# Where the low parts of the experts' weights are computed in an encoder block on one NeuronCore: on VectorE and GpSimd, or on VectorE alone

## The chip, the core and the metric

The kernel runs on one core of one Trainium2 chip. The metric is the device time of one execution in microseconds. The kernel before takes 2730.11 us (median of three runs, 2722.38 to 2731.14). One execution was recorded by the profiler; all views below are of that one.

## What is computed

An encoder block over 1024 tokens of width 1024: layer norm, input projection, two head groups (a recurrent one and a forgetting attention), output projection, layer norm, and then a mixture of experts. The last is where this study plays:

```python
logits = xt @ router_w + router_b
top_val, top_idx = lax.top_k(logits, 4)          # of 32 experts
gates = softmax(top_val)
hid = xb @ w1[e] + b1[e]                         # 1024 -> 2048, for the tokens xb of expert e
x_glu = minimum(hid[..., ::2], 7); x_lin = clip(hid[..., 1::2], -7, 7)
act = x_glu * sigmoid(1.702 * x_glu) * (x_lin + 1)
out = act @ w2[e] + b2[e]                        # 1024 -> 1024
y = sum over a token's experts of gate * out
```

A layer norm of the residual and y follows. All of it is in float32.

## The kernel before

The program has a projection stage, the two head groups, an output projection with the router, the expert stage (about 1043 to 2680 us of the profiled execution) and the last layer norm.

**Exact products from split numbers.** PE multiplies in a rounded float32 format. To keep the accuracy, each factor is split into a high part (a rounding cast) and a low part (the number less its high part), and three products are summed: high by high, high by low, low by high. For activations ScalarE casts the high part from PSUM and VectorE subtracts (`xh`, `xl`, `ah`, `al`, L1148 and L1149). For weights ScalarE casts `wh` from `raw` (L1178), and `wl` = `raw` - `wh` is subtracted at L1181.

**The stream of weights.** The weights of the 32 experts are 384 blocks of [128, 2048] (1 MB each): eight blocks for an expert's first product, four for its second. `weights(j, ahead)` gives block j. It issues loads up to six blocks ahead (`RB`) on SyncE's queue, and it issues the casts and subtractions of the blocks up to j + 3 (`AH`) ahead of block j's matmuls. `wh` and `wl` have four buffers each (`WB`), so the cast of a block waits until PE has done with the block four before. Which engine subtracts is set by a set `pool` of block numbers, from two lists of places in an expert, `POOL_H` and `POOL_L`: 113 of the 384 go to GpSimd, the rest to VectorE.

**Slots and extra slots.** Each expert gets 128 slots for tokens. The 18 experts with the most tokens (`NH`) get 32 extra slots (`CX`); the order of the experts (`SEQ`) spreads these among the others. The extra rows don't use split factors: PE multiplies them straight from `raw` with 32 columns (`ex`, L1199 and L1253). Blocks of tokens beyond the slots are handled by a loop at the end.

**Turns.** The expert stage is written out by hand, without a scheduler. Turn r is the first product of expert r (`up`, eight blocks, steps 0 to 7), then the second product of expert r-1 (`down`, four blocks, steps 8 to 11). Small work is hung on steps: `plan(r, where, f)` puts f behind block `where` of turn r. The activation of expert r has a part for the extra rows (`gx`, `lx`, straight after the first product), and two halves (`gm`, `lm`; L1215 to L1219) at steps 8 and 9 (`DP`), each of which reads half of the first product's PSUM (`h`). Its transposes follow at steps 11, 13 and 14 (`TP`). The next turn's first matmuls (L1190, the bias by a one-hot `sel`) write `h` again and so wait until both halves have been read.

The slots of expert r+2 are worked out in turn r. `begin2` at step 6 makes the one-hot `oh` (L1135) and `sel` (L254). `third` at step 8 (`SLP`) has PE sum what is in the slots (`slots`, L1015 and L1021), VectorE copy it out (`st`, L1030, `sv`, L1005) and compute row numbers, and GpSimd gather the tokens (L1010). For an expert with extra slots, `extra` then turns the extra slots' values (L1027, a matmul that reads `st`), again with `sv`, row numbers and a gather behind it. It stands `SLE` = 1 step later, at step 9. All these matmuls and the transposes write the same PSUM tile `tr`, one buffer, so each waits until the one before has been read.

**Queues.** Every engine works in the order in which its instructions were issued. GpSimd has the subtractions of its blocks, the gathers, and the adding scatters of the results (L1271, L1280).

**The biases of the first product** are split into three exact bfloat16 parts before the expert stage (L259 to L269): two halves of 1024 columns, each with three copies of the biases on 96 partitions. GpSimd subtracts, ScalarE casts, on one group of 32 partitions at a time.

Of the kernel before, what the change touches and what calls it, by code (L numbers as in the profile page):

```python
# [14 lines left out]
OP = mybir.AluOpType  # L15
# [20 lines left out]
NE = 32  # L36
# [4 lines left out]
# the order of work, as ranks by falling count: those with extra slots spread among the others  # L41
SEQ = (0, *sorted(range(1, NE - 1), key=lambda r: (r + 0.5) / NH if r < NH else (r - NH + 0.5) / (NE - NH)), NE - 1)
# the expert that comes first whatever its count, so that its weights can be there early
# [4 lines left out]
SLE = 1  # L48
# [16 lines left out]
POOL_H = (2, 8, 9, 11)  # L65
POOL_L = (0, 10, 11)
# [5 lines left out]
def hybrid_kernel(ctx: ExitStack, tc: tile.TileContext, A, out):  # L72
# [179 lines left out]
    def select(pick):  # L252
        sel = wr.tile([96, P], BF, name="sel", bufs=2)
        ve.tensor_scalar(sel, ons, pick, None, op0=OP.mult)  # L254
        return sel

    first_sel = select(lead_pick)
    # biases of the experts' first product in three exact parts, on 0..31, 32..63 and 64..95
    bh = wr.tile([96, 2 * FF], BF, name="bh")  # L259
    for i in range(2):  # L260
        q = slice(i * FF, (i + 1) * FF)
        b1 = wr.tile([96, FF], FT, name="b1", tag=("xg", "xe")[i])
        for g in range(3):
            sp.dma_start(b1[32 * g:32 * g + 32], A["b1"][:, q])
        ac.copy(bh[:, q], b1)
        for g in (1, 2, 2):
            z = slice(32 * g, 32 * g + 32)
            gp.tensor_tensor(b1[z], b1[z], bh[z, q], op=OP.subtract)
            ac.copy(bh[z, q], b1[z])  # L269
# [14 lines left out]
def rsqrt_steps(nc, pool, v, n, scale, eps, name="rq", out=None):  # L284
    """(v * scale + eps) ** -0.5 for a small tile, one step a call: a first guess from the exponent, then three
    Newton steps r * (3 - a * r * r) / 2, whose factors -2, -8 and -512 are left to the end."""
    ve = nc.vector
    a, r, t = (pool.tile([P, n], FT, name=f"{name}_{x}") for x in "art")
    ve.tensor_scalar(a, v, scale, eps, op0=OP.mult, op1=OP.add)  # L289
    yield r  # L290
    ve.tensor_scalar(r.bitcast(I32), a.bitcast(I32), -0.5, 1597463007.0, op0=OP.mult, op1=OP.add)  # L291
    yield
    for c in (3.0, 12.0, 768.0):
        if n == 1:
            ve.scalar_tensor_tensor(t, r, a[:, 0:1], r, op0=OP.mult, op1=OP.mult)
        else:
            ve.tensor_tensor(t, r, r, op=OP.mult)  # L297
            yield
            ve.tensor_tensor(t, t, a, op=OP.mult)  # L299
        yield  # L300
        ve.scalar_tensor_tensor(r, t, c, r, op0=OP.subtract, op1=OP.mult)  # L301
        yield
    ve.tensor_scalar(r, r, -1.0 / 8192.0, None, op0=OP.mult)
    yield
# [10 lines left out]
def layer_norm2(nc, pool, x, w, b, name, bufs=2):  # L315
    """Layer norm with the scaling on the scalar engine and the last addition on GpSimd."""
    ve = nc.vector
    stt = pool.tile([P, 2, 6], FT, name="ln_st")
    ve.bn_stats(stt[:, 0], x[:, 0:512])
    ve.bn_stats(stt[:, 1], x[:, 512:1024])  # L320
    mv = pool.tile([P, 2], FT, name="ln_mv")
    ve.bn_aggr(mv, stt)
    rs = rsqrt(nc, pool, mv[:, 1:2], 1, 1.0, LN_EPS)
    nm = pool.tile([P, 1], FT, name="ln_nm")
    ve.scalar_tensor_tensor(nm, mv[:, 0:1], -1.0, rs, op0=OP.mult, op1=OP.mult)
    h = pool.tile([P, D], FT, name=name, bufs=bufs)
    nc.scalar.activation(h, x, AF.Identity, bias=nm, scale=rs)
    ve.tensor_tensor(h, h, w, op=OP.mult)
    nc.gpsimd.tensor_tensor(h, h, b, op=OP.add)
    return h  # L330
# [161 lines left out]
def rw_prep(tc, A, L):  # L492
# [16 lines left out]
    # columns at or after the row (inclusive), then strictly after  # L509
# [37 lines left out]
    # inverses of the 16-wide diagonal blocks, four blocks a partition  # L547
# [265 lines left out]
def post_mix(tc, A, L):  # L813
# [60 lines left out]
    def half():  # L874
# [16 lines left out]
        # on 0..31 and 32..63 the high parts, on 64..95 the low ones  # L891
# [22 lines left out]
    def route(t, h1):  # L914
# [29 lines left out]
        # position of the token among those of its expert  # L944
# [13 lines left out]
        # the gate in three exact parts  # L958
# [8 lines left out]
    def rest(t, h1, G):  # L967
        """The sum's start: the residual and the gated biases."""
        n = slice(t * P, (t + 1) * P)
        b2 = L["b2"]  # L970
        ps = ps3.tile([96, P], FT, name="sm")
        for i in range(3):
            pe.matmul(ps[32 * i:32 * i + 32], G, ident, start=True, stop=True)
        gt = p3.tile([96, P], FR, name="gt")
        ac.copy(gt, ps)
        ve.tensor_tensor(gt[32:64], ps[32:64], f32(gt)[32:64], op=OP.subtract)
        yi = p3.tile([P, D], FT, name="yi", bufs=YIB)
        for c in range(2):
            q = slice(512 * c, 512 * c + 512)
            ps = ps3.tile([P, 512], FT, name="sm")  # L980
            pe.matmul(ps, gt, b2[:, q], start=True, stop=True)
            ve.scalar_tensor_tensor(yi[:, q], h1[:, q], ALPHA, ps, op0=OP.mult, op1=OP.add)
        sp.dma_start(ya_d[n, :], yi)
# [5 lines left out]
    # rows beyond the tokens, one a slot, for the slots nobody fills  # L989
# [7 lines left out]
    def slots(pv, oh, n, pq, tag, wr):  # L997
        """What the slots of an expert hold: gates, rows of the tokens, the tokens."""
# [19 lines left out]
        if nh == 2:  # L1018
# [5 lines left out]
            def extra():  # L1024
                """Four copies of the extra slots, one to a group of columns."""
                ps = pq.tile([P, 6], FT, name="slots", tag=tag)
                pe.matmul(ps, st.rearrange("c g s -> c (g s)"), ident[0:6, 0:6], start=True, stop=True)  # L1027
                fill(ps, 1, xe, CX)
# [20 lines left out]
    def rank():  # L1049
        """Experts by falling count, with FIRST before all."""  # L1050
# [10 lines left out]
        # bt[e, f]: e goes before f  # L1061
# [21 lines left out]
    def table():  # L1083
        """Blocks of tokens beyond the slots: partition i holds the expert and the first position of block i."""
# [30 lines left out]
def experts(tc, A, L):  # L1115
# [3 lines left out]
    with ExitStack() as cx:  # L1119
# [18 lines left out]
        def turn(src, name):  # L1138
            """Pieces of work that transpose [128, 1024] and split it into high and low parts."""
# [25 lines left out]
        stream, raws, highs, ready, pool = [], L["raws"], L["highs"], [], set()  # L1165

        def weights(j, ahead):
            """Block j of the stream; loads and splits run ahead of it."""
# [4 lines left out]
            while len(ready) < min(j + 1 + ahead, len(stream)):  # L1173
# [7 lines left out]
                (gp if i in pool else ve).tensor_tensor(l, raw, f32(h), op=OP.subtract)  # L1181
# [39 lines left out]
        def act(ps, px):  # L1221
            """Pieces of work, two halves and the extra rows, each followed by its transposes."""
# [103 lines left out]
        for r in range(NE + 1):  # L1326
            if r < NE:
                at["u", r] = len(stream)
                pool |= {len(stream) + k for k in (POOL_H if SEQ[r] < NH else POOL_L) if k < KD}
                stream += [lambda r=r, k=k: w1(expert(r))(k) for k in range(KD)]  # L1330
            if r:
                at["d", r - 1] = len(stream)
                if r < NE:
                    pool |= {len(stream) + k - KD for k in (POOL_H if SEQ[r - 1] < NH else POOL_L) if k >= KD}
                stream += [lambda r=r, b=b: w2(expert(r - 1))(b) for b in range(4)]
        with tc.manual_schedule():
            info[0] = None, None, CAP, L["first_sel"]
            pool.add(0)
# [45 lines left out]
        # blocks beyond the slots, as many as the routing left  # L1384
        n = nc.values_load(L["tot"][0:1, 0:1], min_val=0, max_val=NE)
        with tc.For_i(0, n, 1) as i:
# [20 lines left out]
            pool.clear()  # L1407
# [63 lines left out]
def host(inputs):  # L1471
# [31 lines left out]
    # columns in four blocks of 256 gate columns and their 256 linear ones  # L1503
# [19 lines left out]
```

## Time and profile before

| | |
|---|---|
| median of three runs | 2730.11 us |
| span of the profiled execution (first to last instruction) | 2735.9 us |
| PE busy | 2431.1 us, 89% of the span |
| VectorE (DVE) busy | 2030.5 us, 74% |
| ScalarE (ACT) busy | 1312.5 us, 48% |
| GpSimd (POOL) busy | 1016.6 us, 37% |
| mean rate of the DMAs | 222 GB/s |

The execution's own time is not given beside its span; the span is 5.8 us above the median. In the tables of instructions a row names line, engine, operation, what it writes and reads, the number of instructions, their busy time and the mean of one, and the idle time of the engine just ahead of them with what ended it. A row of the timeline has start and duration in us; in brackets stands the idle time ahead of it. Matmuls overlap: the distance of their starts, not their duration, is what one costs.

### The profile page before, as it was taken

How to read it: one execution, taken by the hardware profiler on the slowest of the kernel's cores; microseconds unless marked ns; L12 is line 12 of the kernel's file. 1: busy time of each engine (PE TensorE's matmuls, PEld its weight loads, DVE VectorE, ACT ScalarE, POOL GpSimd, SP SyncE). 2: the span in 40 equal slices, each digit the busy share in tenths (PEclk: the TensorE clock that was granted, in tenths of full speed). 3: DMA queues.
4: the chain of work that ended last, by engine and by line, in shares of the span. 5: the costliest groups of instructions: out<-in, count | busy, mean ns of one | idle time of the engine just before them, and what ended most of it. 6: DMA issues, size and time to landing. Idle time of an engine off the chain costs nothing. (4 is left out here: it accounts for less than half of the span.)

```text
span 2735.9 us, 37357 instructions
## 1 busy us (share of the span) xinstructions
PE 2431.1 (89%) x14029; PEld 1803.7 (66%) x14029; DVE 2030.5 (74%) x2816; ACT 1312.5 (48%) x1576; POOL 1016.6 (37%) x489
## 2 busy tenths in 40 slices
PE   5999998899989877899999899998999989999981
PEld 5778998887767654565666666655666656656651
DVE  8377253558876876788779888878798788887676
ACT  3344423544443333455555556554655556555551
POOL 4301111212211133444545456355454455445442
PEclk9999999999999977999999999999999999999995
DMA  6324862245545246587777877876877777877764
GB/s 219 127 94 147 297 167 59 82 156 193 193 162 185 78 181 214 172 309 272 250 264 268 284 288 265 304 258 224 296 287 285 253 261 280 312 272 249 278 240 151
DMA packets 184650, 607.14 MB, mean 222 GB/s; under 512 B 69962, under 2 KB 95690, under 8 KB 130835
## 3 DMA queue, kind: packets, MB, share of 16 engines
q1 hardware_dynamic: 155874, 525.24, 52.5%
q0 software_dynamic: 17600, 65.55, 8.8%
q10 hardware_dynamic: 10992, 13.93, 1.6%
q8 instruction: 112, 1.84, 0.3%
q14 instruction: 72, 0.58, 0.1%
HBM read 518.64 MB, written 86.02 MB: 221 GB/s over the span
## 5 line engine op out<-in xcount | busy, mean ns | idle before, releaser
L1178 ACT CAST wh<-raw 128x2048 fp32r<-128x2048 f32 x381 | 722.5, 1905 | 227.8 <-DMA raw<-w 163.3
L1181 DVE TENSOR_TENSOR wl<-raw,wh 128x2048 fp32r<-128x2048 f32 x271 | 632.7, 2348 | 189.1 <-ACT wh L1178 187.6
L1181 POOL TENSOR_TENSOR wl<-raw,wh 128x2048 fp32r<-128x2048 f32 x113 | 576.1, 5112 | 528.8 <-ACT wh L1178 513.3
L1206 PE MATMUL h<-wh,xh 128*128 128x512 f32 x1024 | 305.8, 421 | 4.5 <-ACT wh L1178 4.5
L1206 PE MATMUL h<-wl,xh 128*128 128x512 f32 x1024 | 283.6, 399 | 0.3 <-DVE wl L1181 0.3
L1206 PE MATMUL h<-wh,xl 128*128 128x512 f32 x1024 | 281.7, 397 | 0.0
L1206 PEld LDWEIGHTS h<-wh,xh 128*128 128x128 f32 x1024 | 183.5, 192 | 81.2 <-issue 25.7
L1206 PEld LDWEIGHTS h<-wl,xh 128*128 128x128 f32 x1024 | 194.4, 190 | 48.0 <-DVE wl L1181 1.0
L1206 PEld LDWEIGHTS h<-wh,xl 128*128 128x128 f32 x1024 | 193.6, 189 | 47.1
L153 PE MATMUL mm<-whi,hT_lo 128*128 128x256 f32 x640 | 186.7, 293 | 9.6 <-DVE rq_a L289 5.0
L151 PE MATMUL mm<-whi,hT_hi 128*128 128x256 f32 x640 | 187.6, 294 | 5.4 <-ACT sq L488 4.0
L1218 DVE SCALAR_TENSOR_TENSOR lm<-lm,gm 128x512 f32<-128x512 f32 x64 | 188.0, 2937 | 2.2
L1263 PE MATMUL o<-wh,ah 128*128 128x512 f32 x512 | 186.7, 448 | 0.0
L152 PE MATMUL mm<-wlo,hT_hi 128*128 128x256 f32 x640 | 185.9, 291 | 0.0
L1263 PE MATMUL o<-wl,ah 128*128 128x512 f32 x512 | 173.2, 422 | 0.0
L1263 PE MATMUL o<-wh,al 128*128 128x512 f32 x512 | 171.5, 418 | 0.0
L1216 ACT ACTIVATE sm<-gm 128x512 f32<-128x512 f32 x64 | 40.3, 630 | 262.8 <-DVE gm L1215 262.8
L1199 PE MATMUL ex<-raw,xt 128*32 128x512 f32 x1152 | 151.0, 605 | 0.0
L486 POOL DMA_DIRECT2D fx_d<-fraw x64 | 35.2, 550 | 289.0 <-ACT sq L488 265.9
L1263 PEld LDWEIGHTS o<-wh,ah 128*128 128x128 f32 x512 | 97.0, 207 | 56.4 <-issue 31.5
L153 PEld LDWEIGHTS mm<-whi,hT_lo 128*128 128x128 f32 x640 | 126.5, 198 | 11.6 <-DVE hT_lo L182 5.9
L151 PEld LDWEIGHTS mm<-whi,hT_hi 128*128 128x128 f32 x640 | 127.1, 199 | 8.7 <-ACT sq L488 4.4
(422 smaller groups left out, 4587.8 us busy)
## 6 DMA issues: line engine op xcount, KB each, us to landing
raw<-w SPq DMA_DIRECT2D x384, 1024.0 KB, 7.1
pks<-pk_d SPq DMA_DIRECT2D x16, 1152.0 KB, 6.3
pk_d<-pk POOLq DMA_DIRECT2D x16, 896.0 KB, 5.3
h_d<-h SPq DMA_DIRECT2D x17, 512.0 KB, 2.6
raw<-w_fx ACTq DMA_DIRECT2D x8, 1024.0 KB, 7.0
fx_d<-fraw POOLq DMA_DIRECT2D x64, 128.0 KB, 2.7
qkvo<-fx_d SPq DMA_DIRECT2D x32, 256.0 KB, 5.9
x<-x SPq DMA_DIRECT2D x8, 512.0 KB, 3.8
```

What stands on the lines that cost most here:

```text
L151: pe.matmul(ps, hi[:, k, n], whi[:, k], start=(k == 0), stop=False)
L152: pe.matmul(ps, hi[:, k, n], wlo[:, k], start=False, stop=False)
L153: pe.matmul(ps, lo[:, k, n], whi[:, k], start=False, stop=(k == KD - 1))
L486: gp.dma_start(fx_d[h, t * P:(t + 1) * P, :], raw)
L1178: ac.copy(highs[i], raw)
L1181: (gp if i in pool else ve).tensor_tensor(l, raw, f32(h), op=OP.subtract)
L1199: pe.matmul(px[32 * c:32 * c + 32], xt[:, k], raw[:, m], start=False, stop=(k == KD - 1))
L1206: pe.matmul(ps[:, c], x[:, k], w[:, m], start=False, stop=z)
L1216: ac.activation(sg, g, AF.Sigmoid, scale=SWI)
L1218: ve.scalar_tensor_tensor(l, l, 1.0, g, op0=OP.add, op1=OP.mult)
L1263: pe.matmul(po[:, c], x[:, k], w[:, m], start=(k == 0 and x is ah and w is h), stop=z)
```

## The change

1. All 384 low parts `wl` are subtracted on VectorE. The lists `POOL_H` and `POOL_L` and the set `pool` are gone.
2. `SLE` is 2 in place of 1: the extra slots' part (`extra`) stands one block later, at step 10.
3. `sel`, the one-hot of an expert (96 x 128), is made by ScalarE in place of VectorE.
4. The biases' subtractions move from GpSimd to VectorE, and are made on 64 partitions and then on 32 rather than on three times 32: four subtractions and four casts in place of six and six.

```diff
-SLE = 1
+SLE = 2
...
-POOL_H = (2, 8, 9, 11)
-POOL_L = (0, 10, 11)
...
-        ve.tensor_scalar(sel, ons, pick, None, op0=OP.mult)
+        ac.activation(sel, ons, AF.Copy, scale=pick)
...
-        for g in (1, 2, 2):
-            z = slice(32 * g, 32 * g + 32)
-            gp.tensor_tensor(b1[z], b1[z], bh[z, q], op=OP.subtract)
-            ac.copy(bh[z, q], b1[z])
+        for n in (64, 32):
+            ve.tensor_tensor(b1[:n], b1[:n], bh[:n, q], op=OP.subtract)
+            ac.copy(bh[:n, q], b1[:n])
...
-                (gp if i in pool else ve).tensor_tensor(l, raw, f32(h), op=OP.subtract)
+                ve.tensor_tensor(l, raw, f32(h), op=OP.subtract)
```

The lines that filled and cleared `pool` go with it; line numbers are two to eight smaller after the change. The rest of the diff is comments.

What moves on VectorE, at the end of the first product of an expert with extra slots whose slots' step serves another such expert. Before, from the first slots' `sv` to the extra slots' `sv`:

```order
L1005 COPY sv<-slots 128x6
L1007 SCALAR_TENSOR_TENSOR sa<-sv 128x1
L1008 TENSOR_TENSOR sb<-sv,tsl 128x1
L1009 SCALAR_TENSOR_TENSOR idx<-sa,tsl,sb 128x1
L1011 TENSOR_REDUCE gate<-sv 128x1
L1215 TENSOR_SCALAR gm<-h 128x512
L1217 TENSOR_SCALAR lm<-h 128x512
L1218 SCALAR_TENSOR_TENSOR lm<-lm,gm 128x512
L1219 TENSOR_TENSOR lm<-lm,sm 128x512
L1005 COPY sv<-slots 128x6
```

And after the change, the same stretch:

```order
L1002 COPY sv<-slots 128x6
L1004 SCALAR_TENSOR_TENSOR sa<-sv 128x1
L1005 TENSOR_TENSOR sb<-sv,tsl 128x1
L1006 SCALAR_TENSOR_TENSOR idx<-sa,tsl,sb 128x1
L1008 TENSOR_REDUCE gate<-sv 128x1
L1178 TENSOR_TENSOR wl<-raw,wh 128x2048
L1212 TENSOR_SCALAR gm<-h 128x512
L1214 TENSOR_SCALAR lm<-h 128x512
L1215 SCALAR_TENSOR_TENSOR lm<-lm,gm 128x512
L1216 TENSOR_TENSOR lm<-lm,sm 128x512
L1178 TENSOR_TENSOR wl<-raw,wh 128x2048
L1002 COPY sv<-slots 128x6
```

Two subtractions of weights now stand between the two `sv`, one ahead of the second half of the activation and one behind it; before, GpSimd had those blocks or they stood further back.

On PE, in the second product of that turn, the extra slots' matmul before:

```order
L1263 MATMUL o<-wh,al 128x512 x2
L1027 MATMUL slots<-ident,st 128x6
L1263 MATMUL o<-wh,ah 128x512 x2
L1263 MATMUL o<-wl,ah 128x512 x2
L1263 MATMUL o<-wh,al 128x512 x2
```

and after, up to the transposes of the activation:

```order
L1260 MATMUL o<-wh,al 128x512 x2
L1024 MATMUL slots<-ident,st 128x6
L1260 MATMUL o<-wh,ah 128x512 x2
L1260 MATMUL o<-wl,ah 128x512 x2
L1260 MATMUL o<-wh,al 128x512 x2
L1260 MATMUL o<-wh,ah 128x512 x2
L1260 MATMUL o<-wl,ah 128x512 x2
L1260 MATMUL o<-wh,al 128x512 x2
L1143 MATMUL tr<-ident,lm 128x128 x4
```

The extra slots' matmul now stands one block (six pairs of matmuls) ahead of the transposes; before it stood two blocks ahead of them.

More of the change, by code (lines that the diff above doesn't have):

```diff
@@ L1163, in front @@
             return todo + [piece], (xh, xl, xt)
-        stream, raws, highs, ready, pool = [], L["raws"], L["highs"], [], set()
+        stream, raws, highs, ready = [], L["raws"], L["highs"], []
         def weights(j, ahead):
@@ L1328, in experts @@
                 at["u", r] = len(stream)
-                pool |= {len(stream) + k for k in (POOL_H if SEQ[r] < NH else POOL_L) if k < KD}
                 stream += [lambda r=r, k=k: w1(expert(r))(k) for k in range(KD)]
@@ L1332, in experts @@
                 at["d", r - 1] = len(stream)
-                if r < NE:
-                    pool |= {len(stream) + k - KD for k in (POOL_H if SEQ[r - 1] < NH else POOL_L) if k >= KD}
                 stream += [lambda r=r, b=b: w2(expert(r - 1))(b) for b in range(4)]
@@ L1337, in experts @@
             info[0] = None, None, CAP, L["first_sel"]
-            pool.add(0)
             todo, _ = begin3(0, L["first"])
@@ L1406, in experts @@
             ready.clear()
-            pool.clear()
             parts, turns, a = act(*up(0, select(pick), *x))
```

## The prediction

> **What bounds the kernel now.** I read the page first, then the waits of the expert stage (1050 to 2700 us), then the engines' timelines around one expert.
>
> ```profile
> span 2735.9 us, 37357 instructions
> ...
> L1178 ACT CAST wh<-raw 128x2048 fp32r<-128x2048 f32 x381 | 722.5, 1905 | 227.8 <-DMA raw<-w 163.3
> L1181 DVE TENSOR_TENSOR wl<-raw,wh 128x2048 fp32r<-128x2048 f32 x271 | 632.7, 2348 | 189.1 <-ACT wh L1178 187.6
> L1181 POOL TENSOR_TENSOR wl<-raw,wh 128x2048 fp32r<-128x2048 f32 x113 | 576.1, 5112 | 528.8 <-ACT wh L1178 513.3
> ```
> ```profile
> 1500.00:2000.00 500.00, 464.36 (x2391) 310.71 (x2389) 415.74 (x332) 278.46 (x216) 244.49 (x66) 0.96 0.77 278
> ```
>
> The second fence is 500 us in the middle of the expert stage (columns: PE, its weight loads, VectorE, ScalarE, GpSimd, granted clock, DMA share, GB/s). PE is busy for 464 of them, VectorE for 416. So PE sets the pace, and what counts is what makes it wait. The expert stage, 1050 to 2700 us, by group of matmuls (last column: PE's idle time ahead of them):
>
> ```profile
> L1027 PE MATMUL slots<-ident,st 6*128 6x6 f32 x34 | 9.1, 337 | 89.1 <-DVE sv L1005 89.1
> L1190 PE MATMUL h<-bh,sel 96*128 96x512 bf16 x124 | 33.1, 390 | 10.1 <-DVE lm L1217 10.1
> ```
>
> Both wait for VectorE, and 89.1 us stand ahead of the extra slots' matmul alone (17 times). Why is VectorE late there, when it has 17% of its time free? One expert's boundary (PE, then GpSimd, VectorE, ScalarE):
>
> ```profile
> 1732.55 1.92 PE L1199 MATMUL ex<-raw,xt 128*32 128x512 f32 x16
> 1738.92 0.63 PE L1263 MATMUL o<-wh,al 128*128 128x512 f32 x2
> 1739.86 0.63 PE L1263 MATMUL o<-wl,ah 128*128 128x512 f32 x2
> 1747.42 0.56 PE L1027 MATMUL slots<-ident,st 6*128 6x6 f32 x2 [6.47 <-DVE sv L1005]
> 1747.91 1.22 PE L1263 MATMUL o<-wh,ah 128*128 128x512 f32 x2
> 1748.93 1.05 PE L1263 MATMUL o<-wl,ah 128*128 128x512 f32 x2
> 1755.70 1.03 PE L1190 MATMUL h<-bh,sel 96*128 96x512 bf16 x4
> ```
> ```profile
> 1732.89 5.55 POOL L1181 TENSOR_TENSOR wl<-raw,wh 128x2048 fp32r<-128x2048 f32 x1 [12.88 <-ACT wh L1178]
> 1741.17 4.50 POOL L1181 TENSOR_TENSOR wl<-raw,wh 128x2048 fp32r<-128x2048 f32 x1 [2.74 <-ACT wh L1178]
> 1749.10 4.62 POOL L1181 TENSOR_TENSOR wl<-raw,wh 128x2048 fp32r<-128x2048 f32 x1
> ```
> ```profile
> 1733.91 4.60 DVE L254 TENSOR_SCALAR sel<-ons,pick 96x128 bf16<-96x128 f32 x1
> 1738.43 0.41 DVE L1215 TENSOR_SCALAR gx<-ex 128x256 f32<-128x256 f32 x1
> 1740.08 0.68 DVE L1215 TENSOR_SCALAR gm<-h 128x512 f32<-128x512 f32 x1
> 1741.40 4.82 DVE L1218 SCALAR_TENSOR_TENSOR lm<-lm,gm 128x512 f32<-128x512 f32 x1
> 1746.93 0.27 DVE L1030 COPY st<-slots 6x128 f32<-6x128 f32 x1
> 1747.78 0.68 DVE L1215 TENSOR_SCALAR gm<-h 128x512 f32<-128x512 f32 x1
> 1755.00 0.16 DVE L1005 COPY sv<-slots 128x6 f32<-128x6 f32 x1
> ```
> ```profile
> 1730.89 1.91 ACT L1178 CAST wh<-raw 128x2048 fp32r<-128x2048 f32 x1 [0.62 <-DMA raw<-w]
> ```
>
> GpSimd's subtraction at 1741.17 ends at 1745.67; VectorE's `lm`, begun 0.23 us after it, takes 4.82 us and ends 0.55 us behind it, at 1746.22. `sel` (1733.91) ends at 1738.51, GpSimd's first one at 1738.44. VectorE stands still while GpSimd subtracts. What these two cost alone is their shortest instance (ns, min/median/max):
>
> ```profile
> L1218 DVE SCALAR_TENSOR_TENSOR lm<-lm,gm x64: 691/3788/5268, 1083.1 to 2657.0; 128x512 f32<-128x512 f32 x64
> L254 DVE TENSOR_SCALAR sel<-ons,pick x31: 273/4608/4633, 1048.3 to 2543.0; 96x128 bf16<-96x128 f32 x31
> L1181 DVE TENSOR_TENSOR wl<-raw,wh x271: 2275/2291/6109, 1032.2 to 2667.9; 128x2048 fp32r<-128x2048 f32 x136
> ```
>
> **The change, part by part.** *Load of VectorE.* It takes over 113 subtractions at 2.291 us: +259 us. It gives up standing still: by the medians (3788 - 691) x 64 = 198 us in `lm` and (4608 - 273) x 31 = 134 in `sel`, an upper figure, as some instances are short. These two alone about balance it. So VectorE isn't fuller than before, but its work lies elsewhere: each `wl` now stands in its queue ahead of the activation and the slots.
>
> I call an expert with extra slots long, one without short; turn r is the first product of expert r and then the second of expert r-1. In it the slots of expert r+2 are worked out. The extra matmul exists in 9 long turns after a short one, 3 long after long, 4 short turns, and turn 0.
>
> *Long turn after a short one* (the rows above). PE ends its first product at 1732.55 + 1.92 = 1734.47; call this T. Before, the next turn begins at 1755.70, T + 21.2. After, VectorE's queue is: `wl`, gx part (1740.08 - 1738.43 = 1.65), `wl`, first half (2.7: 1740.08 to 1746.93 without the 4.13 us lost in `lm`), st, sv and the small ones (0.85), `wl`, second half 2.75, `wl`, the extra sv, then PE's transposes of the activation, which write the same PSUM tile and so wait for sv. The `wl` ahead of gx needs the cast at 1730.89, ends about T + 1, and gx begins there. The next `wl` needs a cast (1.9) that stands on ScalarE behind gx's sigmoid (0.9 after gx begins): it runs from T + 3.8 to 6.1. First half to 8.8, st and sv to 9.7, `wl` to 11.9, second half; the last `wl` needs a cast behind the second sigmoid (11.9 + 1.3 + 1.9 = 15.1) and ends at 17.4; sv 17.5. PE has at T: four blocks of second product of 2.8 us (six pairs of matmuls, 0.47 apart: 1738.92 and 1739.86 are two pairs apart) and 1.1 us of slots: it reaches the extra matmul at T + 9.1, where st (9.0) is just there, and the transposes at T + 12.4. There it now waits about 5 us. The next turn begins at T + 17.9: 3.3 us sooner. One thing comes on top: after the 6.47 us wait the pairs run 0.85 us apart (1747.91, then 1748.93 and 1.05 long) where 0.47 is usual, a dip of between 1 and 2 us that lies within the 21.2; after the new wait the dip falls into the next turn's first product. I take 1.7 us. Left: about 1.4 x 9 = 12 us; bounds -1 (gx 1.7 later, as where raw lands late) and 5 (no dip) each.
>
> The Trainium skill (TensorE: Matmul & The Clock Gate, Part 1: The HAM clock gate) says that an idle window of about 3.4 us halves the clock until a busy one has passed: an estimate of 1.7 us lost for each such wait, so by the page, too, the new wait pays the dip that the old one paid and the sum stays; were the new wait cut below the window, the sum would be 9 x 1.7 us better. The rows show half speed after 6.47 us; for the new waits of 1 to 2 us below I charge no dip, a choice.
>
> *Short turn with an extra matmul, and long after long.*
>
> ```profile
> 1779.99 1.09 PE L1206 MATMUL h<-wh,xl 128*128 128x512 f32 x4
> 1805.77 1.04 PE L1190 MATMUL h<-bh,sel 96*128 96x512 bf16 x4
> ```
> ```profile
> 1681.92 1.09 PE L1206 MATMUL h<-wh,xl 128*128 128x512 f32 x4
> 1700.20 1.04 PE L1190 MATMUL h<-bh,sel 96*128 96x512 bf16 x4
> ```
> ```profile
> 1888.23 1.92 PE L1199 MATMUL ex<-raw,xt 128*32 128x512 f32 x16
> 1914.13 1.04 PE L1190 MATMUL h<-bh,sel 96*128 96x512 bf16 x4
> ```
>
> The first pair is a short turn with the extra matmul: 24.7 us from the end of the first product to the next turn. The second is one without, in which PE never waits: 17.2. After the change the same walk (no gx part; the cast of the last block waits for the end of the first product, so `wl` ends at T + 4.5, first half 7.3, sv 8.1, `wl` 10.4, second half 13.1, `wl` 15.8, sv 16.0) meets a PE that has 1 us of the long expert's second product in each block (eight small matmuls) and comes to the transposes at T + 15.2: 0.8 us of waiting. 17.2 + 0.7 for the extra slots' matmuls + 0.8 = 18.7, a gain of 6.0 x 4 = 24 us. Long after long (third pair, T = 1890.15): 24.0 now; the long turn's queue (sv at 17.5) against a PE at 15.3 makes 17.9 + 2.2 = 20.1: 3.9 x 3 = 12 us.
>
> *The other waits.* `h` behind lm (10.1 us, five times): the half that it waits for is now read at T + 13.2 against a PE at 12.4, so half of it goes: 5 us. The last expert:
>
> ```profile
> 2625.61 0.69 PE L1240 MATMUL tr<-ident,lx 128*128 128x128 f32 x2 [4.46 <-DVE al L1149]
> 2664.00 1.11 PE L1146 MATMUL tr<-ident,lm 128*128 128x128 f32 x4 [5.11 <-DVE al L1149]
> ```
>
> Both follow halves that stood behind GpSimd; with a dip each about 12 us go. The table of left-over blocks (turn 1) stands behind the same stops, SyncE waits for it and holds the loads behind it back:
>
> ```profile
> 1145.41 2.07 PE L1206 MATMUL h<-wh,xh 128*128 128x512 f32 x4 [4.55 <-ACT wh L1178]
> ```
>
> This wait and its dip make 6.3; turn 1's own end stands behind the same stops. I take 8, bounds 0 and 15.
>
> *Biases and sel.* GpSimd's six subtractions go, four on VectorE come:
>
> ```profile
> 1010.60 12.90 POOL L268 TENSOR_TENSOR b<-b,bh 32x1024 f32<-32x1024 f32 x6 [3.88 <-ACT bh L265]
> 1032.23 6.11 DVE L1181 TENSOR_TENSOR wl<-raw,wh 128x2048 fp32r<-128x2048 f32 x1
> ```
>
> Four of 1024 elements at half a `wl` of 2048 (1.15 us) make 4.6 us, of which three and their casts stand ahead of the last router's sums: about 4 us later. The router's small steps behind them stood still beside GpSimd's 12.90 us, as `lm` does, and no longer do: 0 to 5 us back. I take it as even. At 1032.23 one `wl` took 6.11; two now take 4.6 ahead of the first tokens' split: 1.5 to 2 us gained. Turn 0: about 1. Together 3. ScalarE pays 31 small `sel` (taken as VectorE's 0.27 us) and is busy for 278 of 500 us; they stand between casts that are needed three blocks later: nothing, at most 8 us. The gather that now starts a block later has seven blocks until its transposes: nothing.
>
> Sum: 12 + 24 + 12 + 5 + 12 + 8 + 3 = 76 us: 2735.9 - 76 = 2660 for the profiled execution's span. The median of the three runs, 2730.11, is 6 us below that span; what lies around the span isn't shown, so I take the difference off the median: **2654 us**.
>
> **The rivals.** *The wait only moves* (0.15). If each new wait at the transposes is as long as the old one (casts late: ScalarE waits 163 us for loads in this stage), the long turns give nothing and the short ones half: 76 - 12 - 12 - 12 = 40, so 2690. *All goes* (0.10). If the casts come early enough, PE never waits at a boundary: 8.3 x 9 for the first term (21.2 - 12.9), 6.8 x 4 and 6.1 x 3 for the next two, 10 for `h`, 23 for the rest: 153 us, so 2577. For it: the casts' data have mostly landed; against it: ScalarE's order, which puts each cast behind a sigmoid.
>
> *Slower* (0.08): VectorE becomes the bound in the 14 short turns. There PE needs 25.4 us for the first product (1755.70 to 1781.08) and 17.2 for the boundary: 42.6. VectorE is busy for 416/500 of a turn of some 50 us (1755.70 to 1805.77), 41.6 us, and its load stays. If each of its twelve `wl` then also waits 0.7 us for a cast (189.1 us ahead of 271 now), it needs 50.0, 7.4 us more than PE: 104 - 76 = 28 us slower, 2758. It decides from 76/14 = 5.4 us per short turn. Against it: in these waits VectorE is three blocks ahead and waits for buffers that PE frees, and PE has 2.8 us a block for 2.3. The Trainium skill (Perfetto Trace Analysis, Optimizing Scalar/DVE Operations) speaks for this rival: it advises moving work off a saturated VectorE, though it adds that GpSimd, which shares a port, might not help. The trace bears out the second half.
>
> **How the numbers follow.** My forecast has 0.67. Its terms' bounds add to some 45 us either way; with the smaller gain it reaches from 2605 to 2700, and what is left out is "all goes" and "slower", 0.18. A change of 0.3% (8 us) is about what a measurement of this kernel tells from none. Faster 0.90 (forecast, both faster rivals, less a little for small sums), same 0.02, slower 0.08.
>
> **What would show it.** No `lm` or `sel` above 1 us; `slots<-ident,st` without idle time ahead; instead a few us ahead of `tr<-ident,lm` from sv in long turns, little in short ones; `wl` at 2.29 x384; PE in short turns without waits for wl. It is wrong if PE waits for `wl` or `wh` inside first products, or if the waits at `tr` stay above 6 us.

## The result and the profile after

The changed kernel takes 2638.44 us (median of four runs, 2635.85 to 2646.81), the kernel before 2730.62 us beside it (2722.38 to 2737.26). The ratio is 0.9676, with a 95% interval of 0.9659 to 0.9692. The forecast was 2654 us. The profiled execution is the slowest of the four, 2646.81 us; that of before took 2737.26.

From the page of the changed kernel, its span and the subtractions of the weights:

```profile
span 2645.1 us, 37325 instructions
...
L1178 DVE TENSOR_TENSOR wl<-raw,wh 128x2048 fp32r<-128x2048 f32 x384 | 876.7, 2290 | 263.4 <-ACT wh L1175 262.5
```

The stretch of 500 us in the middle of the expert stage that was shown of before, with the same columns:

```profile
1500.00:2000.00 500.00, 481.17 (x2477) 326.47 (x2476) 409.54 (x392) 297.51 (x240) 67.89 (x32) 0.98 0.80 290
```

PE is busy for 481 us of it (464 before). VectorE, with all the subtractions, is busy for 410 where it was 416. The reason stands in the durations of the instructions that had stood still (ns, min/median/max):

```profile
L1215 DVE SCALAR_TENSOR_TENSOR lm<-lm,gm x64: 691/692/695, 1085.1 to 2568.5; 128x512 f32<-128x512 f32 x64
L252 ACT ACTIVATE sel<-ons,pick x31: 392/397/407, 1047.8 to 2462.9; 96x128 bf16<-96x128 f32 x31
L1178 DVE TENSOR_TENSOR wl<-raw,wh x384: 2278/2292/2358, 1036.8 to 2579.4; 128x2048 fp32r<-128x2048 f32 x192
```

No instruction of these is stretched any more. What PE waits for is now the extra slots' `sv`, no longer ahead of the extra slots' matmul but ahead of the transposes. From the waits of the expert stage (total us, times, longest):

```profile
ACT wh L1175 <- DMA raw<-w: 149.3, 83, 4.7
...
PE tr L1143 <- DVE sv L1002: 42.2, 13, 4.8
```

One boundary, from a long turn to a short one (PE, then VectorE; it is the boundary that the prediction walks through, turn 13):

```profile
1702.49 1.92 PE L1196 MATMUL ex<-raw,xt 128*32 128x512 f32 x16
1713.62 0.38 PE L1024 MATMUL slots<-ident,st 6*128 6x6 f32 x2
1716.37 0.63 PE L1260 MATMUL o<-wh,al 128*128 128x512 f32 x2
1720.93 1.11 PE L1143 MATMUL tr<-ident,lm 128*128 128x128 f32 x4 [3.93 <-DVE sv L1002]
1721.84 1.91 PE L1187 MATMUL h<-bh,sel 96*128 96x512 bf16 x4
1723.19 2.27 PE L1203 MATMUL h<-wh,xh 128*128 128x512 f32 x4
```
```profile
1704.66 0.42 DVE L1212 TENSOR_SCALAR gx<-ex 128x256 f32<-128x256 f32 x1
1707.36 2.29 DVE L1178 TENSOR_TENSOR wl<-raw,wh 128x2048 fp32r<-128x2048 f32 x1 [0.96 <-ACT wh L1175]
1710.88 0.69 DVE L1215 SCALAR_TENSOR_TENSOR lm<-lm,gm 128x512 f32<-128x512 f32 x1
1713.14 2.28 DVE L1178 TENSOR_TENSOR wl<-raw,wh 128x2048 fp32r<-128x2048 f32 x1
1718.51 2.29 DVE L1178 TENSOR_TENSOR wl<-raw,wh 128x2048 fp32r<-128x2048 f32 x1 [0.37 <-ACT wh L1175]
1720.72 0.16 DVE L1002 COPY sv<-slots 128x6 f32<-128x6 f32 x1
```

T is 1704.41. `lm` takes 0.69 us (4.82 before), PE meets the extra slots' matmul at T + 9.2 without waiting, then stands for 3.9 us ahead of the transposes until `sv` is read, and the next turn begins at T + 17.4 (21.2 before). `sv` is read 1.2 us sooner than the prediction's walk had it (T + 16.3 for 17.5). The next turn's first two groups of four matmuls take 1.91 and 2.27 us where 1.04 and 1.1 are usual: the dip, a stretch in which PE runs at half speed (granted clock 0.50 from 1721 to 1724 us), lies in the next first product.

By stage, from the rows of both traces: the expert stage (first `h<-bh` to the end of the last `o`) takes 1541.9 us in place of 1635.7, 93.8 less.

### The profile page after: what moved, and what is told of

Its sections match the earlier page's. It is cut to its first block, busy times and chain, and to the rows that moved or that the text cites. A ratio compares the mean times of both kernels' runs of the same rounds, so it can differ in the third digit from the quotient of the medians.

```text
span 2645.1 us, 37325 instructions
## 1 busy us (share of the span) xinstructions
PE 2412.6 (91%) x14029; PEld 1787.9 (68%) x14029; DVE 1941.7 (73%) x2901; ACT 1320.5 (50%) x1606; POOL 425.2 (16%) x370
## 4 chain that ended last, share of the span: by engine, by line
PE 40%; DVE 11%; ACT 4%; DMA 3%; issue 3%; SPq 0%; DVEq 0%; ACTq 0%; POOLq 0%
PE h L1203 23%; PE o L1260 6%; DVE wl L1178 6%; PE ex L1196 4%; ACT wh L1175 4%; DMA raw<-w 3%; PE tr L1143 2%; PE ex L1250 2%; PE h L1187 1%; DVE gm L1212 1%; DVE fy L1444 1%; DVE lm L1215 0%; DVE lm L1216 0%; PE tr L1158 0%; DVE lm L1214 0%
## 5 line engine op out<-in xcount | busy, mean ns | idle before, releaser
L1178 DVE TENSOR_TENSOR wl<-raw,wh 128x2048 fp32r<-128x2048 f32 x384 | 876.7, 2290 | 263.4 <-ACT wh L1175 262.5
L1203 PE MATMUL h<-wh,xh 128*128 128x512 f32 x1024 | 311.8, 427 | 1.2 <-ACT wh L1175 1.2
L1203 PEld LDWEIGHTS h<-wh,xh 128*128 128x128 f32 x1024 | 186.9, 195 | 80.3 <-issue 37.1
L1007 POOL DMA_INDIRECT xg<-h_d,idx x32 | 70.5, 2204 | 949.6 <-issue 317.7
L1260 PE MATMUL o<-wh,ah 128*128 128x512 f32 x512 | 171.6, 416 | 0.0
L1260 PE MATMUL o<-wh,al 128*128 128x512 f32 x512 | 161.1, 396 | 0.0
L1260 PE MATMUL o<-wl,ah 128*128 128x512 f32 x512 | 161.0, 395 | 0.0
L150 PEld LDWEIGHTS mm<-wlo,hT_hi 128*128 128x128 f32 x640 | 127.8, 200 | 0.0
L1260 PEld LDWEIGHTS o<-wh,ah 128*128 128x128 f32 x512 | 88.0, 188 | 53.8 <-issue 34.4
L1260 PEld LDWEIGHTS o<-wh,al 128*128 128x128 f32 x512 | 96.2, 188 | 23.3
```

Source lines behind the costliest of these rows:

```text
L150: pe.matmul(ps, hi[:, k, n], wlo[:, k], start=False, stop=False)
L1007: gp.indirect_dma_start(out=x, out_offset=None, in_=h1_d, in_offset=bass.IndirectOffsetOnAxis(ap=idx[0:m, i:i + 1], axis=0))
L1178: ve.tensor_tensor(l, raw, f32(h), op=OP.subtract)
L1203: pe.matmul(ps[:, c], x[:, k], w[:, m], start=False, stop=z)
L1260: pe.matmul(po[:, c], x[:, k], w[:, m], start=(k == 0 and x is ah and w is h), stop=z)
```

## The experiments

Each was timed beside the kernel before on the same chip; the ratio is to that kernel, with its 95% interval. The experiments ran on four chips, on which the kernel before took 2731.7 to 2733.1 us (2730.6 beside the change); the change itself was not timed again there, so differences to its 2638.4 us carry that much doubt. The start of the expert stage differs by up to 12 us between executions of the same code ahead of it (1035.9 to 1047.5 us in the changed kernels that kept the part ahead of it), so the stage's own length is given beside the median.

| kernel | median us | ratio to before | expert stage us |
|---|---|---|---|
| before | 2730.62 | | 1635.7 |
| the change | 2638.44 | 0.9676 (0.9659 to 0.9692) | 1541.9 |
| before, extra slots a block later | 2771.96 | 1.0143 (1.0119 to 1.0167) | 1669.9 |
| the change, GpSimd subtracts as before | 2754.60 | 1.0076 (1.0048 to 1.0104) | 1653.8 |
| the change, extra slots at step 9 | 2615.19 | 0.9565 (0.9540 to 0.9591) | 1519.9 |
| the change, sel and biases as before | 2637.26 | 0.9655 (0.9620 to 0.9689) | 1538.8 |
| and GpSimd subtracts in vain | 3050.31 | 1.1152 (1.1120 to 1.1184) | 1945.2 |
| and GpSimd fills a tile | 2641.73 | 0.9659 (0.9631 to 0.9688) | 1542.2 |
| transposes at 12, 13, 14 | 2626.01 | 0.9596 (0.9567 to 0.9624) | 1522.3 |
| transposes at 12, 14, 15 | 2599.91 | 0.9505 (0.9477 to 0.9534) | 1495.9 |
| transposes at 12, 14, 16 | 2598.18 | 0.9511 (0.9487 to 0.9534) | 1491.7 |
| two subtractions twice | 2681.63 | 0.9817 (0.9791 to 0.9843) | 1582.1 |
| eight quarters twice | 2675.74 | 0.9796 (0.9762 to 0.9831) | 1577.6 |

### The later extra slots alone

The kernel before with the second part of the change:

```diff
-SLE = 1
+SLE = 2
```

> The kernel before with the second part of the change alone: the extra slots' matmul a block later, GpSimd's subtractions kept. Theory A: the extra sv stands in VectorE's queue behind the same stops, so the wait only moves from the extra matmul to the transposes of lm; long turns still take about T + 21: 2725 us, within 0.4% of before (2715 to 2735). Rival B (the later slots bring the gain by themselves): the boundaries fall to T + 18 and the time to 2690 or below.

It is 1.4% slower, which neither theory had. The same boundary (turn 13), PE:

```profile
1764.54 0.56 PE L1027 MATMUL slots<-ident,st 6*128 6x6 f32 x2 [3.99 <-DVE sv L1005]
...
1769.46 0.63 PE L1263 MATMUL o<-wh,al 128*128 128x512 f32 x2
1774.51 1.12 PE L1146 MATMUL tr<-ident,lm 128*128 128x128 f32 x4 [4.42 <-DVE sv L1005]
1775.42 1.91 PE L1190 MATMUL h<-bh,sel 96*128 96x512 bf16 x4
```

The wait did not move, it split. Ahead of the extra slots' matmul 4.0 us are left of 6.5, since PE has one block (2.8 us) more to do there. In the kernel before, two blocks of PE followed, and under them VectorE reached the extra `sv`; now only one follows, and 4.4 us of `sv` show. Each of the two waits here has a dip of its own. Over the nine long turns after short ones the boundaries grow from 188.3 to 208.4 us in all, and the first products behind them from 225.9 to 242.8.

### The change without its first part

The lists and the set of before are put back, so that 113 subtractions are GpSimd's again; the other three parts stay.

```diff
+POOL_H = (2, 8, 9, 11)
+POOL_L = (0, 10, 11)
...
-                ve.tensor_tensor(l, raw, f32(h), op=OP.subtract)
+                (gp if i in pool else ve).tensor_tensor(l, raw, f32(h), op=OP.subtract)
```

> The changed kernel with its first part undone: the 113 subtractions are on GpSimd again; the extra slots stay a block later, sel on ScalarE, the biases on VectorE. Theory A (the stops beside GpSimd are the cost): lm is slow again (median above 3 us) and so is the wait at the transposes; what is left is sel's stop of 4.3 us per turn, which no longer stands ahead of the activation: 2700 us (2685 to 2720). Rival B (sel's move and the later slots carry most of it): 2665 us or less. Rival C (the first part carries all): 2725 to 2735 us.

It is slower than before, by 0.8%: the stops are back, as theory A says, but its number left out what the later extra slots cost. `lm` again, and the waits that it makes:

```profile
L1217 DVE SCALAR_TENSOR_TENSOR lm<-lm,gm x64: 691/3758/5268, 1083.2 to 2673.7; 128x512 f32<-128x512 f32 x64
```
```profile
PE tr L1145 <- DVE sv L1004: 86.6, 18, 6.6
PE slots L1026 <- DVE sv L1004: 23.6, 13, 6.3
```

Against the run above it wins 17 us. It differs from that in `sel` and the biases alone; the stage accounts for 16 of them. So beside a GpSimd that subtracts, taking `sel` off VectorE is worth some 16 us. The first part, in the presence of the others, is worth 2754.6 - 2638.4 = 116 us; alone it was not run.

### The change without its second part

```diff
-SLE = 2
+SLE = 1
```

> The changed kernel with its second part undone: the extra slots' matmul stands at step 9 again, all subtractions stay on VectorE. Theory A (GpSimd's subtractions were the cost; the later extra slots give nothing and even make the new wait): PE waits about 2.7 us ahead of the extra slots' matmul in the nine long turns after a short one, but the extra sv is then read at about T + 14.8, ahead of the transposes, so the 3.8 to 4.8 us wait at the transposes of lm and its clock dip go; the next turn begins at about T + 15.7 where it is T + 17.7 now. 9 x 2 for the boundaries and 9 to 17 for dips: about 2610 us (2600 to 2625). Rival B (the later extra slots are part of the gain, since they spare the wait for st and sv): the wait at the extra matmul comes back at 5 us or more and nothing goes behind it: 2650 to 2690 us.

2615 us, in the range of theory A: the second part costs 23 us within the change too. The boundary of turn 13, PE and then VectorE:

```profile
1692.09 0.35 PE L1024 MATMUL slots<-ident,st 6*128 6x6 f32 x2 [1.99 <-DVE sv L1002]
1692.37 1.22 PE L1260 MATMUL o<-wh,ah 128*128 128x512 f32 x2
1693.39 1.06 PE L1260 MATMUL o<-wl,ah 128*128 128x512 f32 x2
1694.24 1.05 PE L1260 MATMUL o<-wh,al 128*128 128x512 f32 x2
1695.10 0.96 PE L1260 MATMUL o<-wh,ah 128*128 128x512 f32 x2
1695.89 0.62 PE L1260 MATMUL o<-wl,ah 128*128 128x512 f32 x2
...
1699.61 0.60 PE L1143 MATMUL tr<-ident,lm 128*128 128x128 f32 x4
1700.05 1.03 PE L1187 MATMUL h<-bh,sel 96*128 96x512 bf16 x4
```
```profile
1697.36 0.16 DVE L1002 COPY sv<-slots 128x6 f32<-128x6 f32 x1
...
1698.02 4.48 DVE L1178 TENSOR_TENSOR wl<-raw,wh 128x2048 fp32r<-128x2048 f32 x2
```

One block earlier PE waits for the first slots' `st` and `sv`, 2 us here, and behind this wait the pairs of matmuls run 0.8 to 1.0 us apart for four pairs (granted clock 0.51 from 1692.9 to 1695.9 us). But VectorE now reads the extra `sv` ahead of the last two `wl`, at T + 13.7 (T is 1683.63, the end of the first product), and PE runs from there to the transposes without a wait. The next turn's first matmuls are at full speed. The nine boundaries sum to 151.9 us (159.2 in the change), the nine short first products behind them to 224.4 (242.9): most of the gain is the dip that no longer falls into a first product. The three boundaries of long after long lose 4.9 us of it (59.0 in place of 54.1), nearly all in turn 23. In three turns (4, 23 and 25) the wait is 2.7 to 3.3 us, and the boundary is longer by 2.7 us or more; in two of them ScalarE had stood 3.9 and 3.2 us for a late load ahead of a cast.

### Sel and the biases

The change, with `sel` made on VectorE again and the biases split by six subtractions on GpSimd:

```diff
-        ac.activation(sel, ons, AF.Copy, scale=pick)
+        ve.tensor_scalar(sel, ons, pick, None, op0=OP.mult)
...
-        for n in (64, 32):
-            ve.tensor_tensor(b1[:n], b1[:n], bh[:n, q], op=OP.subtract)
+        for g in (1, 2, 2):
+            z = slice(32 * g, 32 * g + 32)
+            gp.tensor_tensor(b1[z], b1[z], bh[z, q], op=OP.subtract)
```

> The changed kernel with its third part and sel undone: sel is made on VectorE again, and the biases are split by six subtractions on GpSimd. Theory A (sel was slow only because it stood beside GpSimd's subtraction; the biases' split hides beside the routers): sel takes 0.27 us, the expert stage is unchanged within 4 us, its start comes 2 to 3 us later: 2641 us (2633 to 2650). Rival B (sel's move to ScalarE is a part of the gain of its own): 2655 us or more.

2637 us, no difference. `sel` takes 0.28 us on VectorE (0.40 on ScalarE in the change). The span from the seventh router's logits to the first matmul of the stage is 37.1 us before, 35.8 here and 34.3 with the change: the biases are worth 1.5 us, the first block's subtraction 1.3.

### GpSimd subtracts in vain

The change, with the two lists of before for the places:

```diff
                 ve.tensor_tensor(l, raw, f32(h), op=OP.subtract)
+                if i in pool:
+                    gp.tensor_tensor(scr, raw, f32(h), op=OP.subtract)
```

> The changed kernel, and GpSimd does the 113 subtractions of before once more in vain, into a tile that nobody reads (same two inputs, two-byte output); VectorE's results are used, its load is that of the changed kernel. Theory A (VectorE stands still while GpSimd subtracts): lm goes back to a median of 3 us or more, some of VectorE's wl take 4 us or more, VectorE's busy time rises by 200 to 500 us and the time goes to 2740 us or more (2720 to 2850), slower than before. Rival B (what was slow is that the blocks that GpSimd subtracts come late, 5.1 us instead of 2.3): nobody waits for these, so 2638 to 2655 us.

It does the work of the change, and GpSimd's results go into a tile (`scr`) that nobody reads. 3050 us: 412 more than the change, and more than the bounds of theory A. Its mechanism holds, though not as it was spread: some `wl` take over 4 us, as it says, but `lm` keeps its short median (19 of 64 stand beside a vain subtraction and take 3.7 to 4.8 us), and `oh` and `lx`, which it did not name, are stopped as well. VectorE (ns, min/median/max):

```profile
L1220 DVE SCALAR_TENSOR_TENSOR lx<-lx,gx x18: 424/3906/4086, 1089.3 to 2901.3; 128x256 f32<-128x256 f32 x18
L1134 DVE TENSOR_TENSOR oh<-ioc,pv x31: 1218/5534/5882, 1053.3 to 2833.3; 128x1280 bf16<-128x1280 bf16 x17, 128x1024 bf16<-128x1024 bf16 x14
L1181 DVE TENSOR_TENSOR wl<-raw,wh x384: 2274/2292/6734, 1033.1 to 2983.3; 128x2048 fp32r<-128x2048 f32 x192
```

VectorE's busy time is 2369.9 us for the same instructions that take 1941.7 in the change: 428 us of standing still (208 in `wl`, 78 in `lx`, 74 in `lm`, 69 in `oh`), and PE's waits behind it are for `sv` (172 us, 48 in the change), `oh` (65) and `ox`, the extra rows' results (53). A vain subtraction also holds the buffers of `raw` and `wh` until it is done; VectorE waits for casts no longer than in the change, though (243 us, 263 there), and ScalarE's casts no longer for loads (138 us, 149 there), so that is not where the time goes.

### GpSimd fills a tile

The same places, with another work for GpSimd:

```diff
+                if i in pool:
+                    gp.tensor_copy(scr[:, 0:16], f32(h)[:, 0:16])
+                    gp.memset(scr, 0.0)
```

> The changed kernel, and at the same 113 places GpSimd reads 16 columns of wh and then fills a 2048-wide two-byte tile with zeros (about 1.8 us, it reads nothing). Theory A (the stops come from two engines that read SBUF at once): lm stays at a median below 0.8 us and the time within 0.4% of the changed kernel's 2638 us (2628 to 2650). Rival B (any GpSimd work on SBUF stops VectorE): 113 stops of up to 1.8 us, lm's median 1 to 2.5 us, 2680 us or more.

2642 us, as theory A says. GpSimd's two instructions, and VectorE's `lm` beside them:

```profile
L1183 POOL CAST scr<-wh x113: 196/2247/2317, 1030.3 to 2555.4; 128x16 bf16<-128x16 f32 x113
L1184 POOL MEMSET scr<- x113: 1803/1804/1807, 1030.6 to 2557.7; 128x2048 bf16 x113
L1221 DVE SCALAR_TENSOR_TENSOR lm<-lm,gm x64: 691/692/696, 1079.6 to 2564.2; 128x512 f32<-128x512 f32 x64
```

The fill neither stops VectorE nor is stopped (43 of the 64 `lm` ran beside one). The small copy, which reads 16 columns, mostly takes 2.2 us: it is now GpSimd that stands until VectorE's `wl`, begun on the same signal, has ended. So it is not GpSimd's being busy that costs, but both reading at once.

### The transposes later

Three kernels of the change, the first with `TP` = (12, 13, 14), the second with (12, 14, 15), and the third:

```diff
-TP = (11, 13, 14)
+TP = (12, 14, 16)
...
-                for w, f in zip(TP, turns):
+                for w, f in zip(TP if r < NE - 1 else (11, 13, 14), turns):
```

> The changed kernel with the transposes of the activation's first half one block later (first block of the next first product), so that they no longer stand behind the extra slots' read. Theory A (the wait at these transposes of 3.8 to 4.8 us and the clock dip behind it, 17 us of longer first products in the nine turns, are what the long turns still lose): both go, 9 x 4.3 + 17 = 55 us: about 2585 us (2575 to 2605), and the following short first products fall from 27.0 to 25.2 us. Rival B (the wait moves on to the next reader, or the longer first products are not a dip but VectorE's late wl): the boundaries shorten by at most 9 x 4.3 and come back as waits for wl: 2615 to 2640 us.

2626 us, in rival B's range. The nine boundaries fall to 12.4 to 13.1 us, without a wait, but the wait goes on to the second half's transposes, behind `al`, and the nine short first products grow from 242.9 to 255.4 us in all:

```profile
PE tr L1143 <- DVE al L1146: 38.8, 21, 4.2
```

> The changed kernel with the activation's transposes at steps 12, 14 and 15: the first half's one block later, as in the run with 12, 13 and 14, and the other two one block later still. Theory A (in the run with 12, 13 and 14 the wait only went on to the second half's transposes, 2.1 us behind al in every short turn and 1.2 in the long ones after long): these waits go, 14 x 2.1 + 4 x 1.2 = 34 us below that run's 2626: about 2592 us (2580 to 2605). Rival B (al is late wherever the transposes stand, because VectorE's wl stand ahead of it): the wait goes on again, 2615 to 2630 us.

2600 us, in the range of theory A. What is left of this wait:

```profile
PE tr L1237 <- DVE al L1146: 13.9, 13, 1.5
```

> The changed kernel with the activation's transposes at steps 12, 14 and 16, and at 11, 13 and 14 for the last expert as in the changed kernel. Against the run with 12, 14 and 15 it takes away what was left there: 1.1 us behind al ahead of the extra rows' transposes in each short turn (14 times, 15 us), and 4.1 us ahead of the last expert's transposes (5 us longer end). Theory A (these are waits of the path): 2600 - 20 = 2580 us (2572 to 2592). Rival B (the wait goes on to the tokens' transposes that stand at the same step): only the last expert's 5 us, 2593 to 2600 us.

2598 us: the intervals of the last two overlap. The waits behind `al` go but for 2.1 us at the last expert, the wait moves to the tokens' transposes as rival B says (behind `ax`, the extra rows' activations), and the stage gains 4.2 us of the 20, 3.8 of them in the last expert:

```profile
PE tr L1143 <- ACT ax L1238: 12.2, 17, 2.0
```

These two are the fastest versions of the study, 5% below before. Their extra slots stand at step 10: with the transposes out of the way, PE waits there, after turn 0, no more than 1.3 us, once.

### More load for VectorE

The change, with a set `dup` that holds blocks 4 and 6 of each short expert:

```diff
+                if i in dup:
+                    ve.tensor_tensor(l, raw, f32(h), op=OP.subtract)
```

> The changed kernel, and VectorE does two of the eight subtractions of each short expert's first product twice (blocks 4 and 6; 28 more wl, 64 us of VectorE, 4.6 us in each of the 14 short turns). Theory A (VectorE is not what a short turn waits for: it is busy for about 38 us of a turn of 42 to 44, and what it waits for casts is slack, not load): 2638 to 2645 us. Rival B (the slower rival of the forecast, VectorE the bound in the short turns, is near: its waits for casts count as load): PE waits for wl inside the short first products, 14 x 4.6 = 64 us: 2680 to 2710 us.

2682 us, rival B's number; but PE does not wait for `wl`. PE's waits, and one place on VectorE (turn 12):

```profile
PE tr L1239 <- DVE al L1146: 24.5, 14, 3.4
PE tr L1143 <- DVE xl L1146: 9.9, 11, 0.9
```
```profile
1642.13 2.29 DVE L1178 TENSOR_TENSOR wl<-raw,wh 128x2048 fp32r<-128x2048 f32 x1 [2.18 <-ACT wh L1175]
1644.46 2.29 DVE L1180 TENSOR_TENSOR wl<-raw,wh 128x2048 fp32r<-128x2048 f32 x1
1646.67 0.68 DVE L1146 TENSOR_TENSOR al<-tr,ah 128x512 fp32r<-128x512 f32 x1
```

The doubled block (line 1180) stands ahead of `al`, which the next transposes wait for, while VectorE itself had stood idle for 2.18 us just before. That could be order or load, so the same load was spread, with all eight blocks of each short expert's first product in `dup`:

```diff
+                if i in dup:
+                    ve.tensor_tensor(l[:, 0:512], raw[:, 0:512], f32(h)[:, 0:512], op=OP.subtract)
```

> The changed kernel with about the same 4.8 us more for VectorE in each short expert's first product as in the run with two blocks twice, but spread: behind each of the eight subtractions a quarter of it once more (512 columns, about 0.6 us). Theory A (the two doubled blocks cost 43 us because one 2.3 us instruction stood ahead of al and one ahead of xl, which the transposes wait for; VectorE's load itself has room, 38 of 43 us): a quarter delays al and xl by 0.6 us at most, the short first products grow by 1 us or less: 2638 to 2655 us. Rival B (VectorE's load is the bound in the short turns, whatever the order): as with the two blocks, 14 x 2.9 = 41 us: 2670 to 2690 us.

2676 us, which is rival B's number again, and A's does not hold; but the time is not where B has it. The nine short first products sum to 244.4 us (242.9 in the change, 265.8 with two blocks twice): inside them, the six quarters that stand there, 3.7 us of VectorE, are nearly free. The loss is at the boundaries, where two quarters stand ahead of the extra `sv`: 171.1 us for the nine (159.2), 62.5 for the three long after long (54.1); the three short first products behind these (6.4) and the last expert (7.0) make most of the rest. In the last expert and in two of these three the quarters do delay `al`: PE waits 4.9, 2.7 and 1.0 us ahead of the extra rows' transposes, where it waited 1.1 us and not at all in the change. One boundary, VectorE:

```profile
1628.20 2.29 DVE L1178 TENSOR_TENSOR wl<-raw,wh 128x2048 fp32r<-128x2048 f32 x1 [0.36 <-ACT wh L1175]
1630.52 0.69 DVE L1180 TENSOR_TENSOR wl<-raw,wh 128x512 fp32r<-128x512 f32 x1
1631.13 0.16 DVE L1002 COPY sv<-slots 128x6 f32<-128x6 f32 x1
```

PE's wait for that `sv` is 5.2 us here (60.5 in all, 42.2 in the change).

## Why the prediction was right, and where it was not

**What bounds it.** The reading held: PE sets the pace, and what cost was VectorE standing still beside GpSimd's subtractions at the boundaries. Subtractions on GpSimd that nobody needs bring the stops back (428 us), a fill of GpSimd's does not, and with the first part undone 116 us are lost again. The Trainium skill (SBUF — State Buffer, Who interferes with whom) has the same: a VectorE instruction with two inputs in SBUF contends with a GpSimd instruction that reads SBUF, not with one that only writes it, and whoever comes first keeps the other out to its end. The rows agree on each of these points (4.82 us of `lm` beside a subtraction, 0.69 beside a fill, 2.2 for GpSimd's 16 columns beside `wl`). `sel`, which reads one tile in SBUF and not two, was stopped as well (4.6 us). The load: VectorE's busy time fell from 2030.5 to 1941.7 us although it took over 259 us. Counting 8 us of `sel` that left and 5 of the biases that came, the stops before were 259 + 89 + 5 - 8 = 345 us. By instruction, `lm` gave back 148 us, `sel` 100, `oh` 38, `lx` 35 and `wl` 16. The prediction's 332 was for `lm` and `sel` alone, by their medians, as if every instance were stopped; they gave 248, which still about balances what came. That VectorE's busy time fell by 89 us on top comes from what the prediction left out.

**The sum.** Term by term, from the rows of both traces (us gained, the prediction's in brackets):

| term | measured | where |
|---|---|---|
| long after short, nine | 12.1 (12) | boundaries 188.3 to 159.2, first products behind them 225.9 to 242.9 |
| short with an extra matmul, four | 26.8 (24) | 24.7 to 18.0 each; no wait is left where 0.8 was expected |
| long after long, three | 18.7 (12) | 24.3 to 18.0 on average; the new wait is 0.6 to 0.7, not 2.2 |
| `h` behind `lm` | 8.1 (5) | the four boundaries ahead, 56.2 to 48.1 |
| the first products behind these `h` waits | 6.0 (0) | 35.5 to 34.0, four times |
| last expert | 11.8 (12) | 31.5 + 35.5 to 25.4 + 29.8 |
| table of left-over blocks | 7.0 (8) | turn 1's boundary 4.3, turn 2's first product 2.7 |
| start and turn 0 | 3.5 (3) | 2.9 and 0.6 |

The terms sum to 94 against the forecast's 76; the medians differ by 92. The main term came out by its own steps: a new wait of about 5 us (3.8 to 4.8), a boundary of T + 17.9 (16.8 to 18.9), a dip of 1.7 us in the next first product (17.0 / 9 = 1.9). The steps that were mis-sized are "long after long", where PE came to the transposes later and VectorE's `sv` earlier than in the walk, by 0.5 us (T + 15.8 for 15.3) and 1.3 us (T + 16.2 for 17.5), and the first products behind the `h` waits. In three of those, transposes had waited 1.4 us for `al` as well, 4.3 of the 6.0 us, and that was not in the list of waits that go.

**The second part.** The prediction took the four parts as one and gave the later extra slots no price of their own. They cost 23 us within the change and 41 in the kernel before (22 and 34 us of the stage). Its walk has the reason: it says that the new wait arises because the extra `sv` stands behind the last `wl`; it did not ask whether the same `sv`, a block earlier, would stand ahead of it. It would have: T + 13.7 in place of T + 16.3.

**Sel and the biases.** `sel` was taken as nothing on ScalarE, and it is nothing (2637.3 against 2638.4). The biases were taken as even; they are worth 1.5 us.

**The rivals.** "The wait only moves" did not come as a whole, but much of the wait did move: in the nine long turns the new one is 3.8 to 4.8 us, 37.5 in all, where the old was 4.3 to 6.8, 51.6 in all, and that term won no more than 12 us. In the short turns the wait is gone. "All goes" takes another edit: with the transposes moved as well, PE does not wait at the boundaries and the time is 2598 to 2600, not 2577. With transposes at 12, 14 and 15 the nine boundaries give 75 us, as that rival's 8.3 x 9 says; most of what is missing lies in the first products behind them (226 to 244 us). "Slower": VectorE as the bound of short turns did not come either, and the two kernels with more load show how far it is. Inside a short first product 3.7 us more, spread, cost 0.2 us a turn, while 4.6 in two pieces ahead of `al` and `xl` cost 2.5 (22.9 / 9). At a boundary two quarters ahead of `sv`, 1.4 us, cost 1.3 (11.9 / 9). So in these nine turns VectorE's order decides more than its load; in the last expert and in two turns behind long after long the quarters delayed `al`, and there load and order were not told apart. The prediction's condition, load plus waits for casts, was not the one that counts: PE did not wait for `wl` in either kernel, 1.1 us in turn 2 apart.

**The clock.** The Trainium skill (TensorE: Matmul & The Clock Gate, Part 1: The HAM clock gate) was drawn on for a window of about 3.4 us behind which the clock is halved, and the prediction charged no dip for waits of 1 to 2 us. The rows after the 1.99 us wait (1692.37 to 1695.10, 0.8 to 1.0 us a pair) speak against such a window as a bound on the wait: half speed came there for four pairs. In the change itself the choice was not put to the test: where the prediction expected waits of 0.8 and 2.2 us, there were none and 0.6 to 0.7.

## What to carry to other kernels

When an engine's short instructions have a median several times their minimum, look at what the engine beside it does in just that stretch: moving work to a second engine can cost the first more than the work was worth. When a small step that others wait for shares a queue with long ones, count what stands ahead of it at each place it could take; here one place earlier was worth more than the step's own data being ready. And price the parts of a change one by one: the best part here hid a part that lost.

## What the runs showed of the hardware

- VectorE and GpSimd stop each other for most or all of an instruction when both read SBUF, in the instructions that were seen: `lm`, `lx`, `oh` and `wl`, which read two tiles there, and `sel`, which reads one. `oh` of 1.5 us became 5.5 beside a vain subtraction; GpSimd's copy of 16 columns took 0.2 us at its shortest and 2.2 as a rule beside `wl`. A fill, which reads nothing, ran in 1.80 us in all of 113 cases.
- VectorE's instructions that read PSUM were not stopped: `lm<-h` took 673 to 685 ns in all of 64 cases in the run with vain subtractions, 19 of them beside one.
- The length of a wait alone does not tell whether PE comes back at half speed. In the change with the extra slots at step 9, behind the seven waits of 1.7 to 2.5 us ahead of the extra slots' matmul there were always some four pairs at half speed, about 1.5 us; behind 2.7 to 3.3 us, six or seven. In six of the seven the half speed began only three to six matmuls after the wait. With the transposes at 12, 13 and 14, behind waits of 2.13 us ahead of the second half's transposes, there were none in eight of nine cases (granted clock 1.00 behind one of them). In the kernel before with the later extra slots, none came in the block behind one wait of 3.35 us. What tells these apart was not tried.
